# A three-part trunk of gMLP, RWKV-7 and SwiGLU on one core: full-height low parts, loads in pieces, and r's first product moved ahead

## The chip, the cores and the metric

The kernel runs on one core of one Trainium2 chip. The metric is the device time of one execution in microseconds. The engines are TensorE (PE, with its weight loads PEld), VectorE (DVE), ScalarE (ACT), GpSimd (POOL) and SyncE (SP, which only issues DMAs here). ACT also issues DMAs: all weight loads stand in its queue.

## The reference

The input is one sequence of 1024 tokens with 1024 channels. Layer 0 mixes with a gMLP block and a multi-scale pool; layer 1 is RWKV-7 time mixing, where this change sits; each layer ends in a SwiGLU block with 2816 hidden channels. Norms are RMS norms with gains.

```python
h = h + hybrid_ab_mixer(rms_norm(h), ...)                      # layer 0
h = h + (silu(n @ w_gate) * (n @ w_up)) @ w_down               # n = rms_norm(h)
# layer 1, on h = rms_norm(h); xx is the shift by one token
xr, xw, xk, xv, xa, xg = [h + xx * mu[i] for i in range(6)]
r = xr @ w_r
wlog = -softplus(-(w0 + tanh(xw @ w1) @ w2)) - 0.5             # decay, rank 64
k = xk @ w_k
v = xv @ w_v
a = sigmoid(a0 + (xa @ a1) @ a2)                               # learning rate, rank 64
g = sigmoid(xg @ g1) @ g2                                      # gate, rank 160
kk = k * k_k, normalised per head;  k = k * (1 + (a - 1) * k_a)
y = wkv7_scan(r, exp(-exp(wlog)), k, v, -kk, kk * a)           # 16 heads of 64, token by token
y = group_norm(y) + bonus(r, k, v)
h = h + (y * g) @ w_o
h = h + swiglu(rms_norm(h));  out = rms_norm(h)
```

## The kernel before

**Halves and layout.** The sequence is cut into two halves, h = 0 and 1, of 512 tokens. Channels lie on the 128 partitions, in 8 tiles (k, or m for outputs); a tile of activations is 128x512. Everything is FP32. A product is made of three matmuls of the fp32r type (`mm3`, L341 to L344): every operand is split into a high part (a copy on ACT, L143) and a low part (what is left, a subtraction on DVE, L144), and high·high, high·low and low·high are summed in one PSUM bank. A dense product of one output tile is therefore 8 x 3 = 24 matmuls.

**Weights.** `push` writes the plan, the list of all weights in the order of their use; `take` hands out the next one. When a weight is taken, the loads of the next two may be issued and the next one is split. The pool `wst` holds three `raw` tiles (as loaded, 512 KB), three `whi` and three `wlo`. So the order of the plan sets the order of the loads (on ACT's queue, L113) and of the splits on ACT and DVE. Activations that come back from memory (`push_act`, `take_act`) go through the same plan in four pieces each, `("y", h)` among them. The order of instructions on each engine is set afterwards by a scheduler that simulates the program; the code's own order is its starting point.

**Stages.** Layer 0 for both halves; then, for h = 0 and 1:
- `project_gate` and `beside`: mixes of hn, the low-rank first factors (decay and learning rate together) and the gate's first factors, beside dense work of the other half. `lowrank` leaves `tw` and `ta` (the high parts, repeated on both 64-partition halves) and `twlo`, whose upper 64 rows are the low part for the decay and whose lower 64 rows the one for the learning rate. `gate` leaves `ghi`, `glo` and `gst`.
- `project(h)` (L890): the gate's second factor first (8 blocks m of 4 matmuls: three with `ghi`/`glo` and one of 96 rows with `gst`), each block copied out of PSUM by ACT into a tile tagged `epx` or `k` and sent to `g_d`. The second factors of decay and learning rate (`w` and `a`) are split with their low parts stacked on the unused 64 rows (L149, L151). Then p = 0 to 7: k's product, four matmuls for decay and learning rate (L992 with 128 rows, L993 with 64 rows), r's product with small matmuls (norms and bonus) between, the element-wise work. Then v. PSUM is split here in 3 banks `mm`, 4 `aux` and 1 `bo`.
- the recurrence (`recur`), beside most of the SwiGLU block of the other half (`drive`). The part beside the recurrence ends with hidden tiles 18 and 19 (h = 0) or with 14 to 16 and 17 (h = 1). After it comes one more group (`G0B[2]`: hidden tiles 20 and 21, `G1A[2]`: 18 and 19): gate, up, gate, up, and then `down`. y, multiplied by the gate, is loaded again here for the output product; its loads are issued well ahead of that, as raw tiles come free.
- between the halves the residual streams H[h] are stored to `h_d` and loaded again.

The events of a SwiGLU block come from `ffn_events`: g and u are products for one hidden tile, d the down product of a group. A hidden tile is sg = silu(g) on ACT, times u on DVE, then split in `hidhi` (ACT, L669) and `hidlo` (DVE, L670).

Behind layer 0's last group stand these lines, which the change touches:

```python
    hn1 = project_norm(1, np_)
    sp.dma_start(h_d[1, 1], H[1])
    reload(hb_pool, 0, h_d[0, 0])
```

## Time and profile before

| | |
|---|---|
| median of 3 runs | 2513.35 us (2510.25 to 2514.17) |
| the profiled execution, its own time | 2509.54 us |
| its span, first to last instruction | 2507.4 us |
| granted TensorE clock, mean | 0.983 |
| PE busy | 2432.2 us (97%), 15735 matmuls |
| DVE busy | 1382.5 us (55%) |
| ACT busy | 909.8 us (36%) |
| DMA | 310.69 MB, 124 GB/s |

A span is the time from the first to the last instruction; the execution's own time is 2.1 us longer here. A matmul's busy time is modelled, since matmuls overlap in the pipe, so the spacing of their starts tells more than their durations. The granted clock is the share of full speed that the throttle gave TensorE. In a timeline row stand the start in us, the duration, the engine, the line, the operation with output<-input, and in brackets the idle time before it with what released it.

### The profile page before, as it was taken

To read this page: it belongs to the slowest core of one execution; us is meant where nothing else is said; L and a number is where in the kernel's file an instruction comes from. 1 tells how busy PE (TensorE), PEld (TensorE's weight loads), DVE (VectorE), ACT (ScalarE), POOL (GpSimd) and SP (SyncE) were. 2 spreads that over 40 slices of the span, in tenths; PEclk is the share of its full clock that TensorE was granted. 3 is DMA by queue.
4 is the path that set the end of the run, shared out by engine and by line. 5 is a ranking of instruction groups with operands and counts; after the bars stand their busy time and mean duration, and the time that the engine had idled before them with its cause. 6 is when DMAs were issued, how large, how long until landed. Compare 5 with 4: busy or idle time off the path is not lost.

```text
span 2507.4 us, 37920 instructions
## 1 busy us (share of the span) xinstructions
PE 2432.2 (97%) x15735; PEld 1985.9 (79%) x15735; DVE 1382.5 (55%) x2126; ACT 909.8 (36%) x1367; POOL 240.0 (10%) x258
## 2 busy tenths in 40 slices
PE   8999999999999999999999999989999999999998
PEld 6888888888777777787877777768788878888887
DVE  6445634444865964555457846865654445444344
ACT  6233323223663432333225643433333224323223
POOL 0200000000013400121000023301110000100001
PEclk9999999999999998999999999999999999999999
DMA  5113433323355577433334455684544232433231
GB/s 177 47 59 93 143 110 112 107 83 119 91 171 138 135 208 187 144 101 94 124 118 139 143 164 132 165 226 126 168 123 134 85 108 76 151 96 114 92 93 58
DMA packets 434955, 310.69 MB, mean 124 GB/s; under 512 B 93216, under 2 KB 395424, under 8 KB 433760
## 3 DMA queue, kind: packets, MB, share of 16 engines
q10 hardware_dynamic: 297280, 210.53, 28.0%
q1 hardware_dynamic: 137504, 97.75, 13.9%
q8 instruction: 123, 2.02, 0.3%
q14 instruction: 48, 0.39, 0.1%
HBM read 254.68 MB, written 53.54 MB: 123 GB/s over the span
## 4 chain that ended last, share of the span: by engine, by line
PE 79%; DVE 8%; DMA 7%; ACT 2%; issue 2%; SPq 1%; POOL 1%; ACTq 0%; POOLq 0%; DVEq 0%
PE mm L343 22%; PE mm L342 22%; PE mm L344 22%; PE sm L1161 4%; DVE wlo L144 2%; DMA raw<-in_ffn_w_up_dram 1%; PE yp L1161 1%; DMA lnw<-in_rwkv_ln_w_dram 1%; DMA iat<-at_d 1%; DVE xi L1115 1%; DMA raw<-in_ffn_w_down_dram 1%; DVE it L1110 1%; DMA raw<-n_d 1%; DMA ar<-ar_d 1%; DVE alo L144 1%
## 5 line engine op out<-in xcount | busy, mean ns | idle before, releaser
L342 PE MATMUL mm<-ahi,whi 128*128 128x512 f32 x1952 | 766.7, 393 | 3.7 <-DVE h L421 2.9
L343 PE MATMUL mm<-alo,whi 128*128 128x512 f32 x1952 | 769.2, 394 | 0.1
L344 PE MATMUL mm<-ahi,wlo 128*128 128x512 f32 x1952 | 766.8, 393 | 1.7 <-DVE wlo L144 1.7
L143 ACT ACTIVATE whi<-raw 128x1024 fp32r<-128x1024 f32 x288 | 304.3, 1057 | 763.2 <-PE mm L343 604.3
L144 DVE TENSOR_TENSOR wlo<-raw,whi 128x1024 fp32r<-128x1024 f32 x288 | 358.6, 1246 | 312.1 <-ACT whi L143 298.1
L342 PEld LDWEIGHTS mm<-ahi,whi 128*128 128x128 f32 x1952 | 368.1, 189 | 85.6 <-issue 4.7
L343 PEld LDWEIGHTS mm<-alo,whi 128*128 128x128 f32 x1952 | 368.4, 189 | 81.2 <-issue 4.0
L344 PEld LDWEIGHTS mm<-ahi,wlo 128*128 128x128 f32 x1952 | 368.1, 189 | 81.3 <-DVE wlo L144 3.0
L343 PE MATMUL mm<-hidlo,wdhi 128*128 128x512 f32 x624 | 246.2, 395 | 1.0 <-DVE hidlo L670 0.9
L344 PE MATMUL mm<-hidhi,wdlo 128*128 128x512 f32 x624 | 245.4, 394 | 0.0
L342 PE MATMUL mm<-hidhi,wdhi 128*128 128x512 f32 x624 | 239.4, 394 | 5.6 <-ACT hidhi L669 5.6
L421 DVE TENSOR_TENSOR h<-h,mm 128x512 f32<-128x512 f32 x192 | 129.5, 685 | 149.8 <-PE mm L344 149.1
L143 ACT ACTIVATE wdhi<-raw 128x1024 fp32r<-128x1024 f32 x82 | 86.4, 1057 | 265.4 <-DMA raw<-in_ffn_w_down_dram 160.2
L144 DVE TENSOR_TENSOR wdlo<-raw,wdhi 128x1024 fp32r<-128x1024 f32 x82 | 101.5, 1239 | 120.7 <-ACT wdhi L143 120.6
L666 DVE TENSOR_TENSOR sg<-sg,mm 128x512 f32<-128x512 f32 x88 | 60.2, 685 | 160.6 <-PE mm L344 160.5
L342 PEld LDWEIGHTS mm<-hidhi,wdhi 128*128 128x128 f32 x624 | 117.3, 189 | 33.3 <-ACT hidhi L669 7.7
L343 PEld LDWEIGHTS mm<-hidlo,wdhi 128*128 128x128 f32 x624 | 118.3, 190 | 27.4 <-DVE hidlo L670 2.7
L344 PEld LDWEIGHTS mm<-hidhi,wdlo 128*128 128x128 f32 x624 | 118.3, 190 | 24.6 <-issue 0.2
L421 DVE TENSOR_TENSOR hA<-hA,mm 128x512 f32<-128x512 f32 x72 | 48.7, 686 | 77.1 <-PE mm L344 77.1
L347 POOL TENSOR_TENSOR nrs<-nrs,small 128x4 f32<-128x4 f32 x8 | 10.0, 1244 | 675.5 <-DVE nrs L369 675.5
L342 PE MATMUL mm<-xhi,whi 128*128 128x512 f32 (+1 forms) x160 | 65.3, 408 | 2.1 <-ACT k L918 2.1
L670 DVE TENSOR_TENSOR hidlo<-sg,hidhi 128x512 fp32r<-128x512 f32 x88 | 63.3, 721 | 3.0 <-ACT hidhi L669 3.0
(296 smaller groups left out, 2899.6 us busy)
## 6 DMA issues: line engine op xcount, KB each, us to landing
raw<-in_ffn_w_gate_dram ACTq DMA_DIRECT2D x88, 512.0 KB
raw<-in_ffn_w_up_dram ACTq DMA_DIRECT2D x88, 512.0 KB
raw<-in_ffn_w_down_dram ACTq DMA_DIRECT2D x88, 512.0 KB
raw<-in_ab_w_in_dram ACTq DMA_DIRECT2D x16, 512.0 KB
raw<-in_ab_w_out_dram ACTq DMA_DIRECT2D x16, 512.0 KB
raw<-in_rwkv_w_k_dram ACTq DMA_DIRECT2D x16, 512.0 KB
raw<-in_rwkv_w_r_dram ACTq DMA_DIRECT2D x16, 512.0 KB
ar_d<-ar SPq DMA_DIRECT2D x16, 512.0 KB
```

The source lines that it names most:

```text
L143: act.activation(hi, src, AF.Copy)
L144: (eng or dve).tensor_tensor(out=lo, in0=src, in1=hi.bitcast(F32), op=ALU.subtract)
L342: pe.matmul(o, whi, xhi, start=first, stop=False)
L343: pe.matmul(o, whi, xlo, start=False, stop=False)
L344: pe.matmul(o, wlo, xhi, start=False, stop=last)
L347: pool.tensor_tensor(out=t, in0=t, in1=mhalf[:, : t.shape[1]], op=ALU.pow)
L421: dve.tensor_tensor(out=H[h][:, m, :], in0=H[h][:, m, :], in1=o, op=ALU.add)
L666: dve.tensor_tensor(out=s, in0=s, in1=o, op=ALU.mult)
L670: dve.tensor_tensor(out=lo, in0=s, in1=hi.bitcast(F32), op=ALU.subtract)
L1110: dve.tensor_tensor(out=t, in0=bc(iat[:, j, j + 1 : 32].unsqueeze(2), sh), in1=bc(xi[:, j, 0 : j + 1].unsqueeze(1), sh), op=ALU.mult,)
L1115: dve.tensor_tensor(out=xs, in0=xs, in1=t, op=ALU.add)
L1161: i = f(*args, **kw)
```

## The change

It has four parts.

1. *Padded low parts.* The 64-row products of L993 become 128-row products: `twlo` keeps its upper half and gets zeros below, and a new tile `talo` (in the place of `ghi`, which the gate has finished with) gets a copy of the lower half and zeros above. Added per half: one ACT copy of 64x512, two POOL memsets of 64x512.
2. *The gated output bit by bit.* The four pieces of `("y", h)` are planned and taken one behind each g and u of that one group (`G0B[2]`, `G1A[2]`). Before, all four stood in front of its d.
3. *The residual streams bit by bit.* H[1] is stored in eight pieces, each behind its own residual add, and no longer in one transfer of 2 MB; the tile is then used for H[0], which comes back in four pieces.
4. *r's first product in front.* r's product of p = 0 is planned and computed ahead of the gate's second factor, into `o_r`, an `mm` bank that stays taken until p = 0 uses it. The norms of p = 0 then run without a product around them.

```diff
--- before.py
+++ after.py
@@ -208,11 +208,11 @@
             for ff in f:
                 push(("d", l, h, ff), rowblk(ffn_w_down[l], ff * P), dest=whl if lean else lambda: dests["d"]())
 
-    def push_ffn(l, h, groups=GROUPS, before_d=None):
+    def push_ffn(l, h, groups=GROUPS, between=iter(())):
         for e in ffn_events(groups):
-            if before_d is not None and e == ("d", groups[-1]):
-                before_d()
             push_ffn_event(l, h, *e)
+            if e[0] != "d":
+                next(between, None)
 
     def push_lowrank(h):
         for n in range(2):
@@ -226,6 +226,7 @@
         ], lambda t: v3(t)[:, :, :96])
 
     def push_proj(h, nxt):
+        push(("r", h, 0), colblk(rwkv_w_r[0], 0))
         push(("g2", h), rowblk(rwkv_g2[0], 0))
         push(("g2b", 0, h), [(lambda raw, i=i: raw[i * 32 : i * 32 + 32], rwkv_g2[0][128:160, :]) for i in range(3)],
              lambda t: t[:96], lambda: (wst.tile([P, D], F32R, tag="whi", name="whi"),) * 2)
@@ -234,7 +235,8 @@
                  dest=lambda n=n: (dests["wa2"](n),) * 2)
         for m in range(8):
             push(("k", h, m), colblk(rwkv_w_k[0], m * P))
-            push(("r", h, m), colblk(rwkv_w_r[0], m * P))
+            if m:
+                push(("r", h, m), colblk(rwkv_w_r[0], m * P))
         pieces = push_act(*nxt)
         for cb in range(2):
             for kp in range(4):
@@ -291,11 +293,11 @@
     push_beside(0, push_f(0, 1, G0B[0]))
     push_proj(0, ("n0", n_d[0]))
     push_ffn(0, 1, G0B[1])
-    push_ffn(0, 1, G0B[2], lambda: list(push_act(("y", 0), y_d[0])))
+    push_ffn(0, 1, G0B[2], push_act(("y", 0), y_d[0]))
     push_beside(1, push_o(0) + push_f(1, 0, G1A[0]))
     push_proj(1, ("n1", n_d[1]))
     push_ffn(1, 0, G1A[1])
-    push_ffn(1, 0, G1A[2], lambda: list(push_act(("y", 1), y_d[1])))
+    push_ffn(1, 0, G1A[2], push_act(("y", 1), y_d[1]))
     for e in push_o(1):
         e()
     push_ffn(1, 0, G1A[3])
@@ -405,6 +407,7 @@
     def take_act(key):
         for i in range(4):
             take((key, i))
+            yield
 
     def dense_steps(o, whi, wlo, xhi, xlo):
         wh, wl = v3(whi), v3(wlo)
@@ -642,7 +645,7 @@
     l0_es.close()
 
 
-    def ffn(l, h, hn, fp, groups=GROUPS, last=False, nd=3, after=None, before_d=None):
+    def ffn(l, h, hn, fp, groups=GROUPS, last=False, nd=3, after=None, between=iter(())):
         dests["d"] = lambda: (fp.tile([P, D], F32R, tag="wdhi", bufs=nd, name="wdhi"),
                               fp.tile([P, D], F32R, tag="wdlo", bufs=nd, name="wdlo"))
         sg, hid, turned = {}, {}, []
@@ -657,6 +660,7 @@
                 yield from dense_steps(o, *wg, *hn)
                 sg[f] = fp.tile([P, HT], F32, tag="sg", bufs=2, name="sg")
                 act.activation(sg[f], o, AF.Silu)
+                next(between, None)
                 yield FINE / KT
             elif kind == "u":
                 wu = take(("u", l, h, f))
@@ -669,10 +673,9 @@
                 act.activation(hi, s, AF.Copy)
                 dve.tensor_tensor(out=lo, in0=s, in1=hi.bitcast(F32), op=ALU.subtract)
                 hid[f] = (hi, lo)
+                next(between, None)
                 yield FINE / KT
             else:
-                if before_d is not None and f == groups[-1]:
-                    before_d()
                 wd = {}
                 for ff in f:
                     wd[ff] = take(("d", l, h, ff))
@@ -907,6 +910,9 @@
 
         w2 = tmp("w2", 1, [P, D], F32R), tmp("a2", 1, [P, D], F32R)
         dests["wa2"] = lambda n: w2[n]
+
+        o_r = mmt()
+        dense2(o_r, *take(("r", h, 0)), xr)
         g2 = take(("g2", h))
         g2b, _ = take(("g2b", 0, h))
         for m in range(KT):
@@ -920,7 +926,12 @@
                 sp.dma_start(g_d[h][rows[m % 2], m // 2 * 2 + r, :], t[rows[r]])
         for n in range(2):
             take(("wa2", n, h))
-        twa, twlo = (keep["tw"], keep["ta"]), keep["twlo"]
+
+        twlo, talo = keep["twlo"], kp.tile([P, HT], F32R, tag="ghi", name="talo")
+        act.activation(talo[rows[1]], twlo[rows[1]].bitcast(F32), AF.Copy)
+        pool.memset(talo[rows[0]].bitcast(F32), 0.0)
+        pool.memset(twlo[rows[1]].bitcast(F32), 0.0)
+        twa, low = (keep["tw"], keep["ta"]), (twlo, talo)
         smask = tmp("smask", 1, [P, 256])
         pool.memset(smask, 1.0)
         pool.memset(c64(smask)[:, :, 0:1], 0.0)
@@ -988,9 +999,9 @@
             act.activation(kt, o, AF.Copy)
 
             zw, za = auxt(), auxt()
-            for z, w, x, r in ((zw, w2[0], twa[0], rows[0]), (za, w2[1], twa[1], rows[1])):
+            for z, w, x, xl in ((zw, w2[0], twa[0], low[0]), (za, w2[1], twa[1], low[1])):
                 pe.matmul(z, w[:, ms], x, start=True, stop=False)
-                pe.matmul(z, w[r, ms], twlo[r], start=False, stop=True)
+                pe.matmul(z, w[:, ms], xl, start=False, stop=True)
             if prev is not None:
                 late(*prev)
             sg, av = tmp("sg", 2), tmp("av", 2)
@@ -1008,8 +1019,6 @@
             act.activation(epx, cum, AF.Exp, scale=-DEC)
             act.activation(em, cum, AF.Exp, scale=DEC)
             pool.tensor_copy(pct[:, h * 8 : h * 8 + 8, p], c64(epx)[:, :, 63])
-            wr = take(("r", h, p))
-            o = mmt()
             n2 = bo[:, 64 + 8 * p : 72 + 8 * p]
             rn = tmp("rn", 2, [P, 4, 2, 8])[:, 0, 0, :]
 
@@ -1022,7 +1031,13 @@
             small = [lambda j=j: norms(j) for j in range(4)]
             if prev is not None:
                 small += [lambda j=j, pv=prev: bonus(pv[0], pv[3], j) for j in range(4)]
-            dense2(o, *wr, xr, between=small)
+            if p:
+                o = mmt()
+                dense2(o, *take(("r", h, p)), xr, between=small)
+            else:
+                o = o_r
+                for go in small:
+                    go()
             invert_on(INV)
             rb = auxt()
             for j in range(4):
@@ -1521,7 +1536,8 @@
     wp_es.close()
     y, y_es = open_pool(name="y0", bufs=1, side="left")
     ys = open_act(("y", 0), y)
-    drive(ffn(0, 1, nxt["hn"], f, G0B[2], before_d=lambda: take_act(("y", 0))))
+    spill_h = lambda m: sp.dma_start(h_d[1, 1][:, m, :], H[1][:, m, :])
+    drive(ffn(0, 1, nxt["hn"], f, G0B[2], after=spill_h, between=take_act(("y", 0))))
     f_es.close()
     ps_es.close()
     np_, np_es = open_pool(name="np1", bufs=1, side="right")
@@ -1529,8 +1545,10 @@
     ring, ring_es = open_pool(name="ring1", bufs=1, side="right")
     ps_es = open_psum("psd1", DENSE)
     hn1 = project_norm(1, np_)
-    sp.dma_start(h_d[1, 1], H[1])
-    reload(hb_pool, 0, h_d[0, 0])
+
+    H[0] = H[1]
+    for k in range(0, KT, 2):
+        sp.dma_start(H[0][:, k : k + 2, :], h_d[0, 0][:, k : k + 2, :])
     f, f_es = open_pool(name="ffn1b", bufs=1, side="right")
     parts, keep = project_gate(1, hn1, kp, nxt["a"], ring)
     sums = nt.tile([P, HT], F32, tag="nacc", bufs=1, name="nacc")
@@ -1577,7 +1595,7 @@
     act.dma_start(fgb, final_norm.partition_broadcast(P))
     reload(hb_pool, 1, h_d[1, 1])
     ys = open_act(("y", 1), b)
-    drive(ffn(1, 0, hnA, f, G1A[2], before_d=lambda: take_act(("y", 1))))
+    drive(ffn(1, 0, hnA, f, G1A[2], between=take_act(("y", 1))))
     exhaust(out_proj(1, ys))
     hnB = norm_split(1, C_FFN + 8, b)
     drive(ffn(1, 0, hnA, f, G1A[3], last=True))
```

Three places show what this makes of the orders. On PE, at the start of the first `project`, there stands before, among the gate's blocks (w and a are the second factors of decay and learning rate):

```order
L344 MATMUL mm<-ghi,wlo 128x512
L916 MATMUL mm<-gst,whi 128x512 x3
L992 MATMUL aux<-tw,w_5184 128x512
L993 MATMUL aux<-twlo,w_5184 128x512
L342 MATMUL mm<-ghi,whi 128x512
L343 MATMUL mm<-glo,whi 128x512
L344 MATMUL mm<-ghi,wlo 128x512
L916 MATMUL mm<-gst,whi 128x512
L992 MATMUL aux<-ta,a_5185 128x512
L993 MATMUL aux<-twlo,a_5185 128x512
```

and now, from the last matmul of r's product (ahi) on:

```order
L346 MATMUL mm<-ahi,wlo 128x512
L344 MATMUL mm<-ghi,whi 128x512
L345 MATMUL mm<-glo,whi 128x512
L346 MATMUL mm<-ghi,wlo 128x512
L922 MATMUL mm<-gst,whi 128x512
L344 MATMUL mm<-ghi,whi 128x512
L345 MATMUL mm<-glo,whi 128x512
L346 MATMUL mm<-ghi,wlo 128x512
L922 MATMUL mm<-gst,whi 128x512
L1003 MATMUL aux<-tw,w_5182 128x512
L1003 MATMUL aux<-ta,a_5183 128x512
L344 MATMUL mm<-ghi,whi 128x512
```

r's product stands ahead of the gate's blocks, and the low-rank products of p = 0 (tw and ta) follow its second block.

On ACT in the second `project`, from the split of g2b (whi, 96x1024) to the first copies of the gate's blocks (epx and k), there stands before

```order
L149 ACTIVATE whi<-raw 96x1024
L879 ACTIVATE mix<-hn_11006,omv 128x512
L113 DMA raw<-in_rwkv_w_k_dram 128x8x128
L149 ACTIVATE w_11968<-raw 128x1024
L149 ACTIVATE a_11969<-raw 128x1024
L918 ACTIVATE epx<-mm 128x512
L918 ACTIVATE k<-mm 128x512
L918 ACTIVATE epx<-mm 128x512
L143 ACTIVATE whi<-raw 128x1024
```

and now

```order
L149 ACTIVATE whi<-raw 96x1024
L882 ACTIVATE mix<-hn_11018,omv 128x512
L113 DMA raw<-in_rwkv_a_dram 64x1024 x2
L149 ACTIVATE w_11979<-raw 128x1024
L113 DMA raw<-in_rwkv_w_k_dram 128x8x128
L149 ACTIVATE a_11980<-raw 128x1024
L113 DMA raw<-in_rwkv_w_k_dram 128x8x128
L143 ACTIVATE whi<-raw 128x1024
L113 DMA raw<-in_rwkv_w_r_dram 128x8x128
L924 ACTIVATE epx<-mm 128x512
L924 ACTIVATE k<-mm 128x512
L113 DMA raw<-in_rwkv_w_k_dram 128x8x128
```

The copies of the blocks now stand behind the copy of the first k weight (whi), and the load of the second low-rank factor stands inside this stretch.

On ACT at hidden tiles 16 and 17 of layer 1's first half, where the loads for 18 and y are issued (sg is silu of a hidden tile's gate product, ahi a piece of y, hidhi a hidden tile), there stands before

```order
L659 ACTIVATE sg<-mm 128x512
L113 DMA raw<-in_ffn_w_up_dram 128x8x128
L143 ACTIVATE whi<-raw 128x1024
L669 ACTIVATE hidhi<-sg 128x512
L113 DMA raw<-in_ffn_w_gate_dram 128x8x128
L143 ACTIVATE whi<-raw 128x1024
L659 ACTIVATE sg<-mm 128x512
L113 DMA raw<-in_ffn_w_up_dram 128x8x128
L143 ACTIVATE wdhi<-raw 128x1024
L113 DMA raw<-y_d_78 128x1024
```

and now

```order
L662 ACTIVATE sg<-mm 128x512
L113 DMA raw<-y_d_78 128x1024
L143 ACTIVATE ahi<-raw 128x1024
L143 ACTIVATE whi<-raw 128x1024
L673 ACTIVATE hidhi<-sg 128x512
L113 DMA raw<-in_ffn_w_up_dram 128x8x128
L113 DMA raw<-y_d_78 128x1024
L143 ACTIVATE whi<-raw 128x1024
L662 ACTIVATE sg<-mm 128x512
```

Pieces of y now lie between the gate and up weights, the load of the next up weight is issued behind hidhi, and the second sg stands behind that weight's copy (whi).

## The prediction

> **What bounds the kernel now.** I read in this order: busy time by engine, the chain that ended last, the stages the change touches (busy time by stretch), then the matmul timeline inside them with its waits. The first two, from the page:
>
> ```profile
> PE 2432.2 (97%) x15735; PEld 1985.9 (79%) x15735; DVE 1382.5 (55%) x2126; ACT 909.8 (36%) x1367; POOL 240.0 (10%) x258
> ...
> PE 79%; DVE 8%; DMA 7%; ACT 2%; issue 2%; SPq 1%; POOL 1%; ACTq 0%; POOLq 0%; DVEq 0%
> ```
>
> PE is busy for 97% of the span. The other engines count only where PE waits for them, or where its clock falls behind such a wait. Stretches (start:end, length, busy us of PE, PEld, DVE, ACT, POOL with counts, granted clock, DMA share, GB/s), in the order gate's second factor to the end of r's first product (first half), two stretches behind it, y's reload, the gate stretch of the second half, its late project, y's second reload:
>
> ```profile
> 710.82:738.70 27.88, 24.36 (x86) 17.86 (x85) 14.15 (x16) 17.53 (x27) 3.56 (x8) 0.82 0.76 237
> 820.00:876.00 56.00, 52.37 (x366) 40.61 (x366) 54.34 (x100) 28.00 (x42) 24.50 (x18) 0.94 0.53 144
> 928.00:980.00 52.00, 43.76 (x395) 34.66 (x395) 20.35 (x26) 14.14 (x19) 1.90 (x1) 0.87 0.93 235
> 1280.76:1295.51 14.75, 13.11 (x50) 10.00 (x48) 11.11 (x14) 5.71 (x6) 0.00 (x0) 0.88 0.44 138
> 1438.10:1468.05 29.95, 24.90 (x85) 18.22 (x84) 12.57 (x14) 15.76 (x24) 4.01 (x8) 0.83 0.73 227
> 1549.00:1606.00 57.00, 53.16 (x349) 41.66 (x349) 55.33 (x100) 28.25 (x42) 25.92 (x19) 0.91 0.53 145
> 1987.50:2021.10 33.60, 29.77 (x121) 23.29 (x119) 18.06 (x24) 8.07 (x9) 0.00 (x0) 0.95 0.29 91
> ```
>
> A clock of 0.82 over 27.88 us is 5 us of clock lost; the stretch 1280.76 has 14.75 x 0.12 = 1.8 us of it behind a single pair of waits. That is my price of one slow spell.
>
> **Padding.** The matmul timeline around one p (start, duration, engine, line):
>
> ```profile
> 796.06 0.39 PE L344 MATMUL mm<-xhi,wlo 128*128 128x512 f32 x1
> ...
> 796.74 0.39 PE L344 MATMUL mm<-xhi,wlo 128*128 128x512 f32 x1
> 796.97 0.39 PE L992 MATMUL aux<-tw,w 128*128 128x512 f32 x1
> 797.29 0.50 PE L993 MATMUL aux<-twlo,w 64*128 64x512 f32 x1
> 797.72 0.49 PE L992 MATMUL aux<-ta,a 128*128 128x512 f32 x1
> 798.14 0.49 PE L993 MATMUL aux<-twlo,a 64*128 64x512 f32 x1
> 798.56 0.50 PE L342 MATMUL mm<-ahi,whi 128*128 128x512 f32 x1
> 798.90 0.40 PE L343 MATMUL mm<-alo,whi 128*128 128x512 f32 x1
> ```
>
> Equal 128-row matmuls start 0.227 us apart: from 796.06 to 796.97 there are four such steps, two of their rows left out, in 0.91. From 796.97 to 798.90 there are five starts in 1.93 us, where 5 x 0.227 = 1.13 would do: 0.80 us are lost around the two 64-row products. Is it the 64 rows or the change of shape as such? A 96-row product among 128-row ones answers that:
>
> ```profile
> 726.63 0.40 PE L916 MATMUL mm<-gst,whi 96*128 96x512 f32 x1
> 726.87 0.40 PE L342 MATMUL mm<-ghi,whi 128*128 128x512 f32 x1
> ...
> L993 PE MATMUL aux<-twlo,w x16: 498/498/792, 718.2 to 1582.2; 64*128 64x512 f32 x16
> ```
>
> It costs 0.24. The 64-row ones are never under 498 ns in 16. A padded product is an ordinary 128-row one, so I take 0.24 at most for it and a saving of 0.80 per p. Not all 16 p's keep it: p = 0 of each half lies in the gate stretch, counted below; p = 6 and 7 lie in 820–876 and 1549–1606, where DVE is busy 54.34 of 56.00 and 55.33 of 57.00 and sets the pace, so I count nothing there. Left: p = 1 to 5 in two halves, 10 x 0.80 = **8.0** (bounds 0 and 16 x 0.80 = 12.8).
>
> The Trainium skill, "TensorE: Matmul & The Clock Gate", section "Back-to-back issue gap", gives the spacing of isolated warm matmuls as N/2.4 + 2.5 ns, with no term for the rows; by it this edit would save nothing and the sum would be 8.0 smaller. The rows above disagree: 0.43 at 64 rows (797.29 to 797.72) against 0.227.
>
> The added work: one ACT copy of 64x512 and two POOL memsets of 64x512 per half. The nearest rows are an ACT copy of 128x512 (0.57, at 717.66 below) and
>
> ```profile
> L925 POOL MEMSET smask<- 128x256 f32 x2 | 0.6, 314 | 15.8 <-PE mm L343 15.8
> ```
>
> so 0.3 to 0.6 each. Talo takes ghi's place and waits for the gate's last product; its first reader comes behind k's first product, 24 x 0.227 = 5.4 us later, and that hides it. Without that cover it would be about 1.2 us a half.
>
> **r's first product ahead of the gate's second factor.** What waits today, first half (PE, ACT and its queue, DVE), then second half (PE), then a weight's way from issue to its copy:
>
> ```profile
> 713.83 0.96 PE L916 MATMUL mm<-gst,whi 96*128 96x512 f32 x3 [0.81 <-DVE whi L151]
> 717.51 0.79 PE L992 MATMUL aux<-tw,w 128*128 128x512 f32 x1 [2.72 <-DVE w L151]
> ...
> 710.11 1.06 ACT L149 ACTIVATE whi<-raw 96x1024 fp32r<-96x1024 f32 x1 [1.14 <-PE mm L343]
> 713.80 0.40 ACTq L113 DMA_DIRECT2D raw<-in_rwkv_w_k_dram  x1
> 717.66 0.57 ACT L918 ACTIVATE epx<-mm 128x512 f32<-128x512 f32 x1
> 718.62 1.05 ACT L143 ACTIVATE whi<-raw 128x1024 fp32r<-128x1024 f32 x1
> ...
> 712.56 1.22 DVE L151 TENSOR_TENSOR whi<-raw,whi 32x1024 fp32r<-32x1024 f32 x1
> ```
> ```profile
> 1441.39 0.97 PE L916 MATMUL mm<-gst,whi 96*128 96x512 f32 x3 [1.09 <-DVE whi L151]
> 1444.23 0.79 PE L992 MATMUL aux<-tw,w 128*128 128x512 f32 x1 [1.87 <-DVE w L151]
> 1455.42 0.50 PE L342 MATMUL mm<-xhi,whi 128*128 128x512 f32 x1 [2.09 <-ACT k L918]
> ...
> 1979.75 0.39 ACTq L113 DMA_DIRECT2D raw<-in_ffn_w_gate_dram  x1
> 1983.51 1.06 ACT L143 ACTIVATE whi<-raw 128x1024 fp32r<-128x1024 f32 x1 [2.24 <-DMA raw<-in_ffn_w_gate_dram]
> ```
>
> The stretch holds 84 matmuls whichever way they are ordered (32 gate, 4 low-rank, 24 k, 24 r): 84 x 0.227 = 19.1 us. It takes 27.88 and 29.95: 8.8 and 10.9 are lost. r's 24 products now run first, 5.4 us, and cover the split of g2b (1.06 on ACT, 1.22 on DVE). But they hold one of three mm banks, so after blocks m = 0 and 1 (8 x 0.227 = 1.8) the third waits until ACT has copied block 0 out. In ACT's new order that copy stands behind w, a and the first k weight. First half: r from 710.8 to 716.3, two blocks to 718.1. Beside it: g2b's split ends about 713.8, the second low-rank weight is issued then and lands 3.8 later (the last two rows) at 717.6; its copy 1.0, k's copy 1.05 once its load lands at about 719.8, then the block's copy 0.57: 721.4. PE waits 3.2 us net of w's and a's first products, then one slow spell of 1.7, then 0.4 of small waits: 5.3 lost against 8.8, gain 3.5. Second half, same walk from g2b's split at 1441.3: copied out by 1448.5, blocks done at 1445.8, wait 2.7, so 4.8 lost against 10.9, gain 6.1. Together **9.6**. Bounds: all 19.7 if nothing waits; the loss in rival E if each block does. I take the middle walk because every step of it has a row. The norms of p = 0, four small matmuls that ran between r's, take the same PE time as before; new is that they wait for sq (ACT) with nothing beside them, which I count inside the 0.4.
>
> **y bit by bit, first half.** ACT and PE:
>
> ```profile
> 1281.47 1.06 ACT L143 ACTIVATE ahi<-raw 128x1024 fp32r<-128x1024 f32 x1 [4.64 <-DMA raw<-y_d]
> 1283.38 0.62 ACT L669 ACTIVATE hidhi<-sg 128x512 fp32r<-128x512 f32 x1
> ...
> 1284.05 0.98 PE L342 MATMUL mm<-hidhi,wdhi 128*128 128x512 f32 x3 [1.09 <-ACT hidhi L669]
> ```
>
> The hidden tile's copy stands behind y's piece, which waited 4.64 us for its load; PE waits, then runs slowly: 14.75 for 48 x 0.227 = 10.9, 3.9 lost. With pieces taken one by one behind the g and u blocks the copy stands behind one weight only; I leave 0.5 lost: **3.4** (bounds 0 and 3.9).
>
> **y, second half.** 120 x 0.227 = 27.2 in 33.60, 6.4 lost, of which:
>
> ```profile
> 1988.41 0.58 ACT L659 ACTIVATE sg<-mm 128x512 f32<-128x512 f32 x1
> ...
> 2011.95 0.73 PE L342 MATMUL mm<-hidhi,wdhi 128*128 128x512 f32 x2 [2.57 <-ACT hidhi L669]
> ```
>
> 2.57 and its slow spell go. But the activation sg of hidden tile 17, at 1988.41 today, stands in the new order behind the copy of tile 18's u weight, whose load is issued only after tile 16's hidden copy, at about 1987.7: landing 1991.5, weight copy, sg at 1993.3 or later, while PE needs that bank for the third down block from about 1991.6. That is 2.1 idle and 1.7 slow, and behind it tile 17's down product, late by the same loads, is short by an estimated 1.4, with 1.7 slow again: 6.9, with 0.3 small ones 7.2. Net **−0.8** (bounds −4 and +4).
>
> **Residual streams.**
>
> ```profile
> 1350.52 0.32 SPq L1459 DMA_DIRECT2D h<-h_d  x1
> ...
> 1360.81 0.47 PE L342 MATMUL mm<-ahi,whi 128*128 128x512 f32 x1 [1.66 <-DVE h L421]
> ```
>
> One 2 MB reload is issued at 1350.52, behind the whole spill; the residual adds wait for it and PE for their banks: 1.66. In pieces, the first add can go after a quarter: **1.5** (0 to 1.9). Ten more issues on SP at 0.32 us are 3.2 us of a queue that has nothing else there; SP's next transfers would be late only if that reached the first g_d write.
>
> The recurrence is only reordered a little by the scheduler (SP's reload of iat ahead of the memsets' write, PE's bk products eight matmuls later): 0, bounds −6 and +6.
>
> **The sum.** 8.0 + 9.6 + 3.4 − 0.8 + 1.5 = 21.7 less than a span of 2507.4: 2485.7, and with the 2.1 that lies around the span (2509.54 − 2507.4) 2487.8. The profiled run stands 3.8 under the median of 2513.35, whose like would be 2491.6; between them, **2490**.
>
> **Rivals.**
> B, padding worth nothing (2498): the cost is the change of operand or the fp32r pair, not the rows. Against: the 96-row step of 0.24.
> C, the gain is handed back (about 2506): project feeds the recurrence, whose first chunk (928–980) has DMA at 0.93 and PE 8.2 us idle; if its loads end it, project's 8.0 + 9.6 only lengthen that wait, and about 17 − 2 of 21.7 return. Against: the chain gives DMA only 7%, and those loads start earlier too.
> D, better than summed (about 2475): p = 6, 7 keep their 3.2, and the gate stretch loses 2 a half instead of 5, 6 more, the new sg wait does not come, 5 more. The Trainium skill, same page, section "HAM oscillation — how this bites in real kernels", asks for idle gaps over about 3.4 us before the clock falls. Here it is at 0.88 in the stretch whose wait row shows 1.09 (1280.76), so the trace does not agree; by the rule my four slow spells of 1.7 would go, 6.8 more and about 2483.
> E, slower (about 2521): in the gate stretch two banks serve eight blocks, and m = 4 to 7 reuse the epx and k tiles, free only when their g_d writes land. If each waits 3.8 for a landing, 4 x 3.8 + 5 = 20 a half are lost, 40 against 19.7, less the 12.1 from the rest: 8 slower. It decides the sign beyond 0.2% from 18.4 lost a half. For: 1455.42 already waits 2.09 for such a copy. Against: it is the one wait of this kind that PE shows in the sixteen blocks.
>
> **How the numbers follow.** 0.2% is 5.0 us, about what this measurement tells from no change: faster is under 2508.3, slower over 2518.4. Chances: my sum 0.57 (2480 to 2500), B 0.08, C 0.12, D 0.13, E 0.06, other sums that end within 0.2% 0.04. C falls on both sides of 2508.3, 0.05 and 0.07. Faster 0.57 + 0.08 + 0.05 + 0.13 = 0.83, same 0.11, slower 0.06. The range leaves out half of D below and E with the upper part of "same" above: 2472 to 2508.
>
> **What would show it.** Low-rank steps of 0.23 instead of 0.43; the gate stretch at some 24.5 us instead of 27.9 and 30, with one wait for an ACT copy (epx) in place of the two for DVE; no wait for hidhi at the last down of the first half; a wait for sg at the third down block of the second; no 1.66 wait for h. I am wrong if low-rank steps stay at 0.43, if the gate stretch grows, or if 928–980 grows by what project gives.

## The result, and the profile after

The changed kernel takes 2479.64 us (median of 4 runs, 2477.12 to 2482.90) against 2511.80 (4 runs, 2507.82 to 2514.17): a ratio of 0.9874, 95% interval 0.9858 to 0.9890, or 32 us less. The forecast was 21.7 us less, 2490 us, with a range from 2472 to 2508. The direction and the range held; the sum was 10 us short, and its parts, as the runs below show, were wrong in both directions.

The page of the changed kernel, busy time and chain:

```profile
PE 2406.4 (97%) x15735; PEld 1977.5 (80%) x15735; DVE 1382.7 (56%) x2126; ACT 912.1 (37%) x1369; POOL 244.6 (10%) x262
...
PE 82%; DMA 6%; DVE 5%; ACT 2%; issue 2%; POOL 2%; SPq 0%; ACTq 0%; POOLq 0%; DVEq 0%
```

The same 15735 matmuls take 26 us less busy time, and DVE's part of the chain falls from 8% to 5%. The stretches that answer to those of before: the gate stretch of the first half, the first chunk of the recurrence, y's reload, the gate stretch of the second half, y's second reload.

```profile
710.08:736.42 26.34, 22.49 (x86) 17.47 (x85) 13.03 (x14) 14.33 (x21) 3.19 (x7) 0.87 0.81 233
921.18:968.40 47.22, 40.65 (x394) 32.32 (x394) 18.30 (x23) 13.51 (x18) 2.35 (x1) 0.93 0.95 254
1259.88:1274.61 14.73, 11.77 (x50) 8.78 (x48) 9.65 (x13) 4.41 (x5) 0.00 (x0) 1.00 0.53 168
1414.05:1440.84 26.79, 23.12 (x86) 17.55 (x85) 11.21 (x12) 12.89 (x18) 3.18 (x7) 0.87 0.80 230
1953.71:1990.63 36.92, 31.44 (x120) 23.81 (x119) 20.79 (x27) 9.47 (x10) 0.00 (x0) 0.91 0.41 130
```

The gate stretches are 26.34 and 26.79 us, where I had worked out 24.4 and 23.9; y's first reload is as long as before (14.73 against 14.75), the second 3.3 longer; the first chunk of the recurrence is 4.8 shorter (52.00 before), and nothing in the forecast said so.

To see where the whole difference lies, I put borders at matmuls that stand at the same count in every kernel, and took the time between them from the starts. The row of the kernel before is in us, the others are differences to it, one profiled execution each. "Moved" is the order of r's first product.

| kernel (one profile each) | gate 0 | project 0 | recurrence 0 | y 0 | residual | gate 1 | project 1 | recurrence 1 | y 1 | span |
|---|---|---|---|---|---|---|---|---|---|---|
| before | 33.5 | 136.5 | 405.6 | 39.4 | 113.9 | 34.0 | 137.6 | 385.4 | 55.8 | 2507.4 |
| padding_only | −0.9 | −2.7 | −1.7 | 0.0 | 0.0 | −3.5 | −2.3 | +6.4 | +1.7 | −2.7 |
| y_bits_only | −0.8 | +0.4 | −4.5 | −1.3 | −0.4 | −3.5 | +0.1 | +6.0 | +3.8 | −1.2 |
| residual_bits_only | −0.1 | 0.0 | −6.7 | +0.2 | −1.9 | −1.1 | −0.3 | +4.6 | +1.0 | −4.1 |
| iat_ahead | −0.8 | −0.3 | −6.0 | −0.5 | 0.0 | −2.6 | −0.1 | +3.1 | +0.9 | −7.3 |
| first_product_late | −0.2 | +0.1 | 0.0 | +0.1 | +0.1 | −2.6 | +0.3 | +10.1 | +1.3 | +9.0 |
| both_orders | −0.8 | +0.1 | −7.5 | +0.6 | 0.0 | −1.9 | +0.1 | +11.9 | +1.6 | +3.1 |
| r_first_only (moved) | −0.4 | −1.7 | −9.3 | +0.3 | 0.0 | −3.1 | −1.6 | −3.7 | +0.3 | −20.1 |
| r_before_k (moved) | −0.1 | −1.6 | −14.7 | 0.0 | 0.0 | −3.5 | −1.7 | −3.9 | +3.0 | −22.4 |
| no_padding (moved) | −1.4 | −1.5 | −10.3 | −1.1 | −2.3 | −4.2 | −1.2 | −6.0 | +2.8 | −26.1 |
| no_y_bits (moved) | −1.6 | −4.1 | −11.3 | −0.4 | −1.9 | −3.5 | −3.5 | −3.4 | +1.6 | −28.5 |
| low_rank_early (moved) | +0.6 | −3.0 | −16.4 | +0.7 | −2.3 | −2.5 | −4.2 | −3.9 | +3.2 | −29.5 |
| all_r_before_k (moved) | −1.2 | −4.0 | −15.2 | +0.6 | −2.3 | −1.9 | −3.4 | −2.2 | +3.1 | −26.4 |
| the full change (moved) | −1.5 | −4.6 | −13.9 | −0.8 | −2.3 | −3.2 | −4.1 | −2.7 | +2.9 | −31.5 |

Some readings come first. A stage of the recurrence differs by 4.5 and 6.7 us between kernels with all but the same order of matmuls there (y_bits_only and residual_bits_only against before, recurrence 0), so one cell of these columns proves little. And the profile of the kernel before has two odd stages: its gate 1 is long, since every other kernel is 1 to 4 us shorter there, and its recurrence 1 is short, since the next three rows are 4.6 to 6.4 us longer there. Groups of rows do say something: the two recurrences together take 788.9 to 795.7 us in the first four rows (mean 792.1) and 770.7 to 778.0 in the seven rows with r moved (mean 774.3). That is 17.8 us of the 32.

### The profile page after: what moved, and what is told of

The parts are those of the page before. It is cut to its first block, busy times and chain, and to the rows that moved or that the text cites. A ratio compares the mean times of both kernels' runs of the same rounds, so it can differ in the third digit from the quotient of the medians.

```text
span 2475.9 us, 37980 instructions
## 1 busy us (share of the span) xinstructions
PE 2406.4 (97%) x15735; PEld 1977.5 (80%) x15735; DVE 1382.7 (56%) x2126; ACT 912.1 (37%) x1369; POOL 244.6 (10%) x262
## 4 chain that ended last, share of the span: by engine, by line
PE 82%; DMA 6%; DVE 5%; ACT 2%; issue 2%; POOL 2%; SPq 0%; ACTq 0%; POOLq 0%; DVEq 0%
PE mm L344 22%; PE mm L345 22%; PE mm L346 22%; PE sm L1176 5%; DMA raw<-y_d 1%; DVE wlo L144 1%; PE yp L1176 1%; DMA raw<-in_ffn_w_down_dram 1%; DMA lnw<-in_rwkv_ln_w_dram 1%; ACT whi L143 1%; PE aux L1097 1%; PE mm L511 1%; PE mm L512 1%; PE mm L513 1%; PE aux L1098 1%
```

## The experiments

Each was timed in five rounds against the kernel before on the same chip.

**Each part alone.** The first two:

```diff
# padding_only: the kernel before, with
-                pe.matmul(z, w[r, ms], twlo[r], start=False, stop=True)
+                pe.matmul(z, w[:, ms], xl, start=False, stop=True)
# and talo, the copy and the two memsets
# r_first_only: the kernel before, with
+        o_r = mmt()
+        dense2(o_r, *take(("r", h, 0)), xr)
         g2 = take(("g2", h))
# and r's first weight ahead of g2 in the plan; p = 0 then uses o_r
```

> The kernel before with the padded low parts alone. The ledger by my sum: 8.0 us less, all of it between the end of the first r product and the stretch where DVE sets the pace, 4 us in each half, and the recurrence's stretches as before. The rival reading of the result (two equal sets of matmuls compared at the same count, before against after): 9 to 10 us in the two project stages, and if the 16 us that the two recurrences gained beyond my sum hang on what padding does to the order at project's end, another 10 to 16 us there: 18 to 26 in all.

Measured: 2502.97 against 2508.11 us, ratio 0.9979 (0.9963 to 0.9995): 5 us less, and 2.7 + 2.3 in the two project stages.

> The kernel before with r's first product ahead of the gate's second factor alone, 64-row low parts kept. By my sum 9.6 us less (3.5 and 6.1), recurrence unchanged. By the comparison of the traces 4.8 us less (1.6 and 3.2) in the two gate stretches, because PE then waits there for the second low-rank factor (2.2 us) and for the copy of a gate block (1.6 us) and runs slowly behind it. If the recurrence's 16 us come from this part: 15 to 20 us less.

Measured: 2486.99 us, ratio 0.9922 (0.9904 to 0.9940): some 20 us less, two thirds of the whole change. The gate stretches gave 0.4 and 3.1, project 1.7 and 1.6, the recurrences 9.3 and 3.7. The 9.6 us of my forecast were not in the gate stretches; 13.0 us stood in the recurrences, where I had forecast nothing.

```diff
# y_bits_only: the kernel before, with
+                next(between, None)          # behind each g and u
-                if before_d is not None and f == groups[-1]:
-                    before_d()
# residual_bits_only: the kernel before, with
-    sp.dma_start(h_d[1, 1], H[1])
-    reload(hb_pool, 0, h_d[0, 0])
+    H[0] = H[1]
+    for k in range(0, KT, 2):
+        sp.dma_start(H[0][:, k : k + 2, :], h_d[0, 0][:, k : k + 2, :])
# and the store in eight pieces
```

> The kernel before with the gated output taken bit by bit alone. By my sum 2.6 us less (3.4 gained in the first half, 0.8 lost in the second). By the comparison of the traces 0 to 3 us more: nothing gained in the first half (a wait of 2.4 us stays at its down products) and about 2.8 us lost in the second. The recurrence before it should not change by either.

Measured: 2508.95 us, ratio 1.0010 (0.9999 to 1.0021). In its two stretches 1.3 gained and 3.8 lost.

> The kernel before with the residual streams in pieces alone. By my sum 1.5 us less, by the comparison of the traces 2.3 us less, both at the first residual adds behind the reload, where the wait of 1.66 us for h goes. Nothing in the recurrences, unless the scheduler reorders the second one.

Measured: 2506.90 us, ratio 1.0004 (0.9990 to 1.0017). The stretch behind the reload is 1.9 us shorter, as in every kernel with this part (1.9 to 2.3); the whole time cannot tell so little.

**Where does r's gain lie?** The same product, with no cover given to the gate:

```diff
# r_before_k: the kernel before, with
         for n in range(2):
             take(("wa2", n, h))
+        o_r = mmt()
+        dense2(o_r, *take(("r", h, 0)), xr)
```

> The kernel before, with r's first product planned and computed behind the gate's second factor and the low-rank factors, just ahead of k's first product, and not ahead of the gate. If the part's gain is the cover that r gives the gate stretch, as my prediction had it, this version has none of it: 0 to 3 us less than before. The rival: r's first product alone was worth 19.6 us though the gate stretches gave only 3.5, so most of it comes from the order that the move sets in the recurrences (the first recurrence product stands 118 matmuls behind project's last v product instead of 110). This version's order there is nearly that of r's first product ahead of the gate, so by the rival it is 13 to 18 us faster than before, with PE's wait for bk at the first recurrence product at about 1 us instead of 4.

Measured: 2487.13 against 2510.00 us, ratio 0.9911 (0.9896 to 0.9927). It is as fast as r ahead of the gate, and its gate stretch has the waits of before. PE's waits in it between 700 and 745 us (engine, line, waited for, us in total, times, longest):

```profile
PE aux L996 <- DVE w L151: 2.7, 1, 2.7
PE mm L918 <- DVE whi L151: 0.8, 1, 0.8
```

So the cover that r gives the gate is not what the part is worth. What both versions share is that r's product is gone from its place between k's product and the element-wise work of p = 0.

**Parts taken out of the full change, and one added.**

```diff
# no_padding: the full change with the 64-row products of before
# no_y_bits: the full change with y taken in front of the down products, as before
# low_rank_early: the full change, with w2 and a2 planned behind r's first weight, ahead of g2, and
-        o_r = mmt()
+        o_r = auxt()
# all_r_before_k: the full change, with r's first product where r_before_k has it
```

> The changed kernel with the 64-row low parts of before. If padding is worth what the matmul steps say in the two project stages (0.80 us per p, 8 to 10 us in all), this version is 22 to 24 us faster than before, where the full change is 31.6. If it is worth only the 5.3 us that it gave alone, 26.

Measured: 2485.92 against 2510.00 us, ratio 0.9900 (0.9887 to 0.9914), where the full change has 0.9874 (0.9858 to 0.9890): the intervals just overlap. The project stages say it more sharply: −1.5 and −1.2 without padding, −4.6 and −4.1 with it, 6.0 us for padding.

> The changed kernel with the gated output taken in front of the down products, as before. By my sum it loses 2.6 us against the full change (29 faster than before). By the experiment with that part alone (2.5 us slower) it is 34 us faster than before, and the two stretches where y is loaded again are as before: 39.4 and 30.1 us instead of 38.5 and 33.5.

Measured: 2483.10 us, ratio 0.9892 (0.9878 to 0.9906). The intervals of this and of the full change overlap: whether y bit by bit is worth keeping isn't settled. In y's own two stretches it costs about 1 us (−0.4 and +1.6 without, −0.8 and +2.9 with it).

> The changed kernel with the second factors of decay and learning rate planned right behind r's first weight, ahead of the gate's, and with r's first product in a bank of the four aux banks, so that the gate has its three mm banks. If the two waits in the gate stretch (2.2 to 2.7 us for a's split, 0.8 to 1.6 us for the copy of a gate block) and the slow clock behind them are what keeps it at 26 us where 84 matmuls need 19.1, it gains 3 to 7 us a half against the full change: 38 to 45 us faster than before. If another wait takes their place (the gate's weights, now later in the plan), no more than 2 us in all: 30 to 34.

Measured: 2481.39 us, ratio 0.9890 (0.9873 to 0.9906): no gain over the full change. PE's waits between 700 and 745 us:

```profile
PE mm L344 <- ACT epx L926: 4.1, 1, 4.1
PE mm L924 <- DVE whi L151: 1.9, 1, 1.9
```

The wait for a's split is gone, and one for g2b's split and a longer one for a block's copy stand in its place, although the gate has its three banks again. One late copy was exchanged for another on the same two engines.

> The changed kernel, with r's first product behind the gate's second factor and ahead of k instead of ahead of the gate. By the prediction's theory (r covers the gate stretch) it loses 5 to 10 us against the full change: 22 to 27 faster than before. By the rival (the gain lies in the recurrences, and the gate stretch gave only 3.5) it is within 4 us of the full change: 28 to 35 faster.

Measured: 2481.38 against 2509.76 us, ratio 0.9881 (0.9864 to 0.9898), within the interval of the full change. It makes no measurable difference on which side of the gate r stands, so long as it has left p = 0.

**What changed in the recurrences?** PE's waits in recurrence 0 (876 to 1178 us), first of the kernel before (two rows under 0.6 us left out), then of the full change:

```profile
PE sm L1163 <- DMA bk<-bk_d: 4.3, 1, 4.3
PE sm L1161 <- DVE gt L1208: 3.6, 4, 1.6
PE sm L1161 <- DVE XT L1249: 2.9, 2, 1.9
PE sm L1161 <- ACT akv L1259: 2.3, 1, 2.3
PE sm L1161 <- DVE gch L1375: 1.7, 1, 1.7
```
```profile
PE sm L1176 <- DVE gt L1223: 7.7, 4, 4.6
PE mm L345 <- issue: 0.8, 1, 0.8
PE sm L1178 <- DMA bk<-bk_d: 0.8, 1, 0.8
```

The names waited for are tiles of the recurrence. The waits for bk (the first chunk's load), XT (the result of the inversions) and akv are nearly gone, the one for gt has grown: 9.3 us are left of 15.7.

The stage is not shorter by its waits alone. Recurrence 0 of the kernel before and of the full change, as stretches:

```profile
875.17:1280.76 405.59, 389.89 (x3956) 324.32 (x3957) 220.25 (x416) 124.31 (x211) 38.18 (x34) 0.97 0.50 140
868.24:1259.88 391.64, 382.35 (x3956) 317.77 (x3957) 224.57 (x423) 128.23 (x214) 40.22 (x34) 0.99 0.52 147
```

PE is idle for 15.7 and 9.3 us, and busy for 7.5 us less with the same number of matmuls, at a granted clock of 0.99 instead of 0.97. For both recurrences together, the first four rows of the table against the seven with r moved, PE's idle time is 30.0 us on average against 20.0, and its busy time 762.0 against 754.4. Among the waits, bk's fall from 6.9 to 1.4 us and XT's from 5.2 to 1.8. So of the 18 us some ten are waits, and nearly eight go with a clock that is slow for less of the time. Whether the clock stays up because the waits are fewer is not shown.

The orders differ at two places. On PE the first recurrence product stands 118 matmuls behind project's last v product instead of 110, so that more dense work runs before the wait for bk. On SP the load of iat (the input of the second inversion) stands ahead of the first inversion's write to xi_d, and is out much sooner. SP's queue, before and then in the full change, where a piece of bk_d ahead of these rows is issued 6.9 us earlier (869.90 against 876.75):

```profile
880.63 1.11 SPq L1119 DMA_DIRECT2D xi_d<-xi  x2
881.86 4.32 SPq L954 DMA_DIRECT2D iat<-at_d  x2
927.62 1.12 SPq L1119 DMA_DIRECT2D xi_d<-xi  x2
```
```profile
874.52 1.13 SPq L965 DMA_DIRECT2D iat<-at_d  x2
875.90 1.10 SPq L1134 DMA_DIRECT2D xi_d<-xi  x2
919.25 1.12 SPq L1134 DMA_DIRECT2D xi_d<-xi  x2
```

The two loads are issued by 875.65 instead of 886.18, 10.5 us sooner where a row ahead of them is 6.9 and the last row 8.4 sooner. I set each order by hand in the kernel before, project untouched. In iat_ahead the loads of iat end up between the two halves of the write, at 879.51 to 881.88, and not ahead of both.

```diff
# iat_ahead: the kernel before; the first inversion's write is held back
         dve.tensor_copy(x2[:, :, 1, :], xi.rearrange("p i c -> p c i"))
+        for _ in range(4 if p0 == 0 else 0):
+            yield
# first_product_late: the kernel before; the first product is written later, and
# chained behind the dense matmul that came last until then (mm3 keeps it in dense_last)
-        yield 0.2
+        yield 0.2 + 14.4
+        last.append(dense_last[0])
         gram(0, 0)
# both_orders: both
```

> The kernel before, with the first inversion's write to xi_d held back by a few steps, so that SP issues the load of iat in front of its second half. PE's order keeps the old place of the first recurrence product (111). If the early iat load is what the recurrences gain by, 10 to 17 us faster than before; if PE's order is, within 4 us of before, with PE's wait for bk still at about 4 us.

Measured: 2502.73 against 2509.76 us, ratio 0.9970 (0.9958 to 0.9981): 7 us less. This is the time of the whole kernel; its two recurrences together take 788.1 us, hardly less than the 788.9 to 795.7 of the first four rows, so the stages don't say where the 7 us lie. Its waits in recurrence 0 (876 to 1178) hold none for XT, and bk's is halved:

```profile
PE sm L1163 <- DVE gt L1210: 8.3, 4, 5.6
PE sm L1163 <- DVE uv L1281: 2.2, 1, 2.2
PE sm L1165 <- DMA bk<-bk_d: 2.2, 1, 2.2
```

> The kernel before, its project untouched, r's first product in its old place. Only the recurrence's first product is written later in the code and chained behind a dense matmul, so that it stands 118 matmuls behind project's last v product instead of 110, as in the kernels with r moved. If the 17 us that the two recurrences gain in all kernels with r moved come from the place of that product (dense work in front of the wait for bk, and the order that follows from it), this kernel is 12 to 17 us faster than before, PE's wait for bk about 1 us. If they come from project itself (p = 0's element-wise chain starting a product earlier, the iat load issued ahead of the xi_d write), it is within 4 us of before.

Measured: 2520.23 us, ratio 1.0044 (1.0029 to 1.0058): some 10 us more. In its waits (860 to 1178) bk's is halved as well, and what it gave stands at XT:

```profile
PE sm L1163 <- DVE gt L1210: 5.9, 3, 2.9
PE sm L1163 <- DVE XT L1251: 5.8, 2, 4.2
PE sm L1163 <- ACT akv L1261: 2.1, 1, 2.1
PE sm L1163 <- DMA bk<-bk_d: 2.0, 1, 2.0
```

That makes recurrence 0 equal (0.0). Recurrence 1 is 10.1 longer than in the profile of before (4 to 6 longer than in the next three rows of the table), and not by waits, which are 14.3 us against 14.1. By the starts, PE goes over from a dense matmul to a recurrence product 55 times there and spends 27.1 us in these steps, against 32 times and 21.2 us in the kernel before. The steps back are 3.5 us more as well, and the steps from dense to dense, 23 fewer, are 4.7 less: 4.7 of the 10.1 us come from going to and fro. The other 5.4 stand in the steps from one recurrence product to the next, at a granted clock of 0.98 in this stage against 0.99. Chaining the first product cut the dense work in that half into finer pieces, which I hadn't meant.

> The kernel before, project untouched, with both orders of the kernels with r moved: the first inversion's write held back, so that SP issues the load of iat in front of its second half, and the recurrence's first product 118 matmuls behind project's last v product. Alone the first was 7 us faster and the second 10 us slower, since the product's gain at the wait for bk came back as a wait for XT, the second inversion's result, which the early iat load brings sooner. If these two orders together are what moving r sets free in the recurrences, 12 to 17 us faster than before, bk's wait at 1 to 2 us and none for XT. If more of moving r is needed (p = 0's element-wise work starting sooner), it is no better than the early load alone: 3 to 8 us faster.

Measured: 2511.36 against 2510.78 us, ratio 0.9996 (0.9987 to 1.0005). Recurrence 0 is 7.5 shorter, with bk's wait at 0.2 and XT's at 0.5 (876 to 1178):

```profile
PE sm L1165 <- DVE gt L1212: 8.8, 5, 3.4
PE sm L1165 <- DVE uv L1283: 2.8, 1, 2.8
PE sm L1165 <- DVE XT L1253: 0.5, 1, 0.5
PE sm L1165 <- DMA bk<-bk_d: 0.2, 1, 0.2
```

Recurrence 1 is 11.9 longer, with 61 such changes. So the two orders take away the waits that they were meant for, and the forcing adds time in the second half; whether the first half is faster for it can't be told, since its −7.5 is little more than the −4.5 and −6.7 of kernels with the order of before. What is shown: moving r's first product out of p = 0, on either side of the gate, shortens the two recurrences by 18 us, and holding back the write for an earlier load of iat makes the whole kernel 7 us faster. What stays open: whether these 7 us are a part of the 18, and how the rest divides between the place of the first product, the element-wise work of p = 0, which no longer has r's product beside it, and the many small shifts of dense work that the scheduler makes with it. No kernel here has one of these without the others.

## Why the prediction was right, and where its terms were wrong

**Padding: the step right, the size 8.0 against 5 to 6.** The matmul timeline around one p of the changed kernel, and the tile's row:

```profile
792.62 0.39 PE L1004 MATMUL aux<-twlo,w 128*128 128x512 f32 x1
792.84 0.39 PE L1003 MATMUL aux<-ta,a 128*128 128x512 f32 x1
793.07 0.39 PE L1004 MATMUL aux<-talo,a 128*128 128x512 f32 x1
793.30 0.39 PE L344 MATMUL mm<-ahi,whi 128*128 128x512 f32 x1
...
L1004 PE MATMUL aux<-talo,a x16: 389/389/395, 736.0 to 1550.2; 128*128 128x512 f32 x16
```

0.227 a step and 389 ns instead of 491: rival B is out. The Trainium skill's formula for the spacing of isolated matmuls ("TensorE: Matmul & The Clock Gate", section "Back-to-back issue gap"), which has no term for the rows, does not hold for the 64-row steps here. The 10 x 0.80 us come out at 2 x 3.7 in the part where PE sets the pace (up to the border at p = 6, full change against no_padding), and 0.6 and 0.8 of it are handed back in the stretch where DVE does. I had set that stretch's worth at nothing; it was slightly negative.

**r in front of the gate: the walk nearly right, the gain wrong.** I forecast that PE would stand 3.2 us in the first gate stretch, because the third block's bank waits for ACT's copy until 721.4. It stood for longer, and in two parts, of which the second is this wait:

```profile
719.99 0.50 PE L1003 MATMUL aux<-ta,a 128*128 128x512 f32 x1 [2.23 <-DVE a L151]
722.12 0.80 PE L344 MATMUL mm<-ghi,whi 128*128 128x512 f32 x1 [1.63 <-ACT epx L924]
...
717.63 1.06 ACT L149 ACTIVATE a<-raw 128x1024 fp32r<-128x1024 f32 x1 [1.01 <-DMA raw<-in_rwkv_a_dram]
720.52 1.06 ACT L143 ACTIVATE whi<-raw 128x1024 fp32r<-128x1024 f32 x1 [1.84 <-DMA raw<-in_rwkv_w_k_dram]
721.49 0.58 ACT L924 ACTIVATE epx<-mm 128x512 f32<-128x512 f32 x1
```

a's load was in at 717.6, k's copy began at 720.5 and the block's ended at 722.1: the walk held within 1 us. PE stood 3.9, of which 2.23 were the wait for a's split on DVE, which I had said would be gone, and 1.63 the wait for the copy. In the second half it stood 3.6, again 2.5 of them for a's split. (My walk there was not quite its own: by the steps of the first half the times 1445.8 and 1448.5 come out at 1445.4 and 1448.9, and two first products of 0.227 taken off the first half's 3.3 leave 2.9, not 3.2. That is under 1 us.) Two sizes failed. The slow spell behind the waits was put at 1.7 and is 26.34 x 0.13 = 3.4 us, and about as much in the second half. And the 10.9 lost in the second half before were those of one odd profile: the other kernels without the move are 1.1 to 3.5 us shorter there. Against those the part's two gate stretches gain 1 to 2 us, not 9.6. The step that failed is the subtraction from a single profile of before.

**The recurrences: 0 forecast, bounds ±6, measured −17.8.** I had seen both moved rows, the bk product eight matmuls later and iat ahead of the write, and called them "reordered a little". This is the term that made the sum come out short, and it hid the missing 8 us of the gate. That the total came within 10 us of the forecast is luck: the other terms as measured (5 to 6 for padding, 1 to 2 for the gate, 0.4 and −2 for y, 1.9 for the residual streams) make 6 to 8 us, and with the recurrences at the 0 that I gave them the time would be about 2505. Rival C went the other way than I feared: project's gain was not handed back at the first chunk, whose stretch is 4.8 shorter although the DMA engines are busier (0.95). D's time (2475) was near, for another reason than D's. E did not come: PE waits for a block's copy once in the first half, 1.63 us, and for 1.1 us in all in the second, and not for one landing after another.

**y, first half: 3.4 forecast, about 0.4 measured.** (The y 0 column is −0.4 on average over the five kernels with this part, from −1.3 to +0.7, and 0.0 over the others.) The wait for hidhi did go, from 1.09 to 0.31. Another came. PE, DVE and ACT:

```profile
1262.39 0.96 PE L344 MATMUL mm<-hidhi,wdhi 128*128 128x512 f32 x3 [0.31 <-ACT hidhi L673]
1263.74 0.50 PE L345 MATMUL mm<-hidlo,wdhi 128*128 128x512 f32 x1 [0.38 <-DVE hidlo L674]
1267.67 0.50 PE L344 MATMUL mm<-hidhi,wdhi 128*128 128x512 f32 x1 [2.27 <-DVE h L424]
...
1265.79 1.23 DVE L144 TENSOR_TENSOR alo<-raw,ahi 128x1024 fp32r<-128x1024 f32 x1 [2.11 <-ACT ahi L143]
...
1264.70 1.06 ACT L143 ACTIVATE ahi<-raw 128x1024 fp32r<-128x1024 f32 x1 [2.36 <-DMA raw<-y_d]
```

The next piece's split stands on DVE ahead of the residual adds and waits for that piece's load; the adds free PE's banks. The late load of y moved from ACT's queue, where hidhi stood behind it, to DVE's.

**y, second half: −0.8 forecast, about −2.** (The y 1 column is 1.3 on average over the kernels without this part, before included, and 3.2 over those with it.) Here too the mechanism was as told, with other sizes:

```profile
1958.26 0.50 PE L344 MATMUL mm<-hidhi,wdhi 128*128 128x512 f32 x1 [0.53 <-ACT sg L662]
1981.07 1.65 PE L344 MATMUL mm<-hidhi,wdhi 128*128 128x512 f32 x3 [3.27 <-ACT hidhi L673]
...
1956.67 1.06 ACT L143 ACTIVATE whi<-raw 128x1024 fp32r<-128x1024 f32 x1 [3.52 <-DMA raw<-in_ffn_w_up_dram]
1957.63 0.58 ACT L662 ACTIVATE sg<-mm 128x512 f32<-128x512 f32 x1
1977.44 1.06 ACT L143 ACTIVATE ahi<-raw 128x1024 fp32r<-128x1024 f32 x1 [5.57 <-DMA raw<-y_d]
```

sg stood behind the up weight's copy, and PE waited 0.5 us for it where I had 2.1. The wait for hidhi at tile 17's down product, which I had at 1.4, is 3.3, since a piece of y, for which ACT stood idle for 5.57 us, is ahead of hidhi on ACT.

**Residual streams: 1.5 forecast, 1.9.** The wait for h is gone. SP's twelve issues took 8.20 and 4.27 us, and not 0.32 each as I had it, but the queue's next transfer starts only at 1374.99, 46 us behind them, so they delay nothing there.

## What to carry to other kernels

Where a scheduler sets the order, a moved product is worth what it does to the order of everything behind it. Count the rows that change place in the stages it was not aimed at, and give each a price of its own wait before calling it nothing. Test the cover story by giving the move without the cover: here the version without it was just as fast. And compare a stage with several profiles of before: one stage in one profile was off by up to 7 us, more than most of the terms of the sum.

## What the runs showed of the hardware

A 64-row product among 128-row ones costs 0.42 to 0.43 us a step, and the 128-row product between two of them 0.42 as well, against 0.227 for the padded one; a 96-row product costs hardly more than that (0.24).

The slow clock does not go by the length of the wait alone: 2.23 and 1.63 us of waits at 720 us were followed by a stretch at 0.87, and 0.31, 0.38 and 2.27 us around 1265 us by none (1.00). The Trainium skill ("TensorE: Matmul & The Clock Gate", section "HAM oscillation — how this bites in real kernels") asks for a gap over about 3.4 us; no single wait in the gate stretch was that long, so the rule alone does not tell which waits bring the slow clock.

A step from a dense matmul to the recurrence's small products takes 0.5 to 0.66 us on average with its waits, and nearly doubling their number in recurrence 1 (32 to 61) brought 11 us more in these steps (21.2 to 32.1). With the steps back (3.9 us more) and the 29 dense steps that are missing (5.5 us less) it is 9.3 us, or some 0.3 us for each time that PE goes to and fro.
